# Transposed modulation parts, full-height score operands and head pairs in a two-layer hybrid backbone

## The chip, the cores and the metric

The kernel runs on one core of a Trainium2 chip. The metric is the device time of one execution in microseconds; the median of three runs of the kernel before is 2051.74 us (2051.34 to 2056.99).

## The reference, cut to what matters

The model takes 512 latent tokens and 256 context tokens of width 1024 through two layers. Each layer multiplies and shifts its input by rows that come from a conditioning vector, mixes tokens, normalises, and sends each token to two of 32 experts. The even layer mixes with a bidirectional linear recurrence beside windowed attention (8 query heads of 64, 2 key and value heads, a sink); the odd layer with latent attention (8 heads of 96, 64 for values) beside a depthwise convolution.

```python
def _modulation(cond, w, b):
    m = (jax.nn.silu(cond) @ w + b)[..., None, :]
    return jnp.split(m, 6, axis=-1)

def _modulate(x, shift, scale):
    return x * (1.0 + scale) + shift

# even layer, latent tokens: window of 128 each way, all context keys, one sink
p = jax.nn.softmax(jnp.concatenate([s_win, s_ctx, s_sink], axis=-1), axis=-1)
out = jnp.einsum('bnkgqm,bnmkd->bnqkgd', p_win, vb) + jnp.einsum('bnkgqc,bckd->bnqkgd', p_ctx, v_ctx)
# even layer, context tokens: all context keys and the sink
# odd layer: keys of context and latent tokens, every head of its own
p = jax.nn.softmax(s, axis=-1).astype(v.dtype)
return jnp.einsum('bhqk,bkhd->bqhd', p, v)
```

## The kernel before, in words

**Order.** `forward` (line 1659) runs the even mixer, its output projection and routing, the experts of layer 0, the odd mixer, and the same again. Instructions are written in program order; a planner, which simulates the engines with its own costs, lays out each engine's queue at compile time: it takes ready instructions by priority, the order of writing. On the chip every engine then works through its queue in order. Weights come in pieces of 2 MB through one queue (SP) into a ring of slots (`Stream`); a slot's next transfer starts when the work on it has ended (`done`).

**Modulation.** A section (one of six rows of 1024 per layer and per stream) is computed in two halves. `modulation_rows` (line 213) multiplies the two conditioning columns, padded to 32, with the weights. The contraction over 1024 is cut into four parts, each on its own 32 output partitions, so partition 32c holds part c for the latent stream and 32c+1 for the context. ScalarE copies that bank to SBUF (line 222). `modulation` (line 226) does both halves and gives back `finish`, which is called later: 16 matmuls (line 239) take 64 strided columns of the copy as the weights and `pick`, a 128x2 selector, as the moving operand, so that each adds the four parts and turns 64 features onto partitions. VectorE adds the bias (line 240). Ten sections go this way, six in the even mixer (`fill`, line 495) and four in the odd one (line 1983); the first two sections of layer 0 go through lines 361 to 368 with the same `modulation_rows`. Every f32 matmul in the program is two instructions in the trace, each with its own weight load.

**Heads of the even layer.** `maxima` (line 552) finds each query's row maximum and turns its negative, split into a bf16 pair, onto four partitions, `mT` (line 586). `scores` (line 614) makes one block of scores, keys on partitions: two f32r matmuls with the split queries and keys, one bf16 matmul that adds the maxima (`sel`, four rows, against `mT`, line 637; line 627 for the context's queries), and masks; ScalarE takes exp into a tile `P` (line 643; nine such tiles). `heads` (line 646) takes a pair of heads, t, which share the output banks `ol` and `oc`, head i on partitions 64i to 64i+63. It runs head 0's seven units and then head 1's. `use` multiplies P with the values (line 669, line 661 for the context's queries) two units after the scores, and GpSimd adds P into the head's first P tile (lines 674, 662). `normalise` (line 685) sums over keys with a matmul of ones (line 692), both heads side by side in one bank, adds the sink (line 693), and scales. The loop at line 705 calls it for the pair before, at the eighth step of the next pair.

**Heads of the odd layer.** `operands` (line 1901) makes each head's split queries `qh`, `ql` and keys `kh`, `kl`: 96 rows, and in `qh` and `kh` two more that carry the maxima and ones. The tiles alternate between two pools. `scores` (line 1996) uses 96, 96 and 98 rows (lines 1999 to 2001); lines 1935 and 1940 make the scores for the maxima with 96 rows.

Of the kernel before, what the change touches and what calls it, by code (L numbers as in the profile page):

```python
# [11 lines left out]
F = mybir.dt.float32  # L12
FR = mybir.dt.float32r
# [21 lines left out]
def host_arrays(inp):  # L35
# [6 lines left out]
    a["xT"] = x.reshape(NT, 8, 128).transpose(2, 1, 0)  # L42
    a["wmod"] = i["w_mod"].reshape(2, 128, 8, 12, 512).transpose(0, 3, 1, 2, 4).reshape(2, 12, 128, 4096)
    a["lng"], a["lnb"] = i["ln_g"], i["ln_b"]
# [71 lines left out]
    cf["pick"][0::32, 0] = cf["pick"][1::32, 1] = 1  # L116
    cf["eps"] = np.full((128, 1), EPS)
    F_off, o = {}, 0
    for k, v in cf.items():
# [92 lines left out]

def modulation_rows(K, s):

    nc = K.nc
    q = K.ps.tile([128, 512], F, tag="b", name="qmod")
    for k in range(2):
        for c in range(4):
            nc.tensor.matmul(q[32 * c:32 * c + 32], K.cond[:, 2 * c + k, :],  # L219
                             s[0][:, 1024 * c + 512 * k:1024 * c + 512 * k + 512], start=(k == 0), stop=(k == 1))  # L220
    m = K.mp.tile([128, 512], F, tag="msb", name="msb", bufs=2)
    nc.scalar.activation(m, q, AF.Copy)
    return m


def modulation(K, l, sec):

    nc = K.nc
    ms = []
    for b in range(2):  # L230
        s = K.stream.get(("mod", l, sec, b))
        ms.append(modulation_rows(K, s))
        K.stream.done(s)

    def finish():
        t = K.ps.tile([128, 512], F, tag="b", name="fmp")
        for b in range(2):
            for j in range(8):
                nc.tensor.matmul(t[64 * b:64 * b + 64, 2 * j:2 * j + 2], ms[b][:, j::8], K.cst["pick"], start=True, stop=True)
        nc.vector.tensor_tensor(K.fm[:, l, :, sec], t[:, 0:16].rearrange("p (j i) -> p i j", j=8),  # L240
                                K.fmb[:, l, None, sec].to_broadcast([128, 2, 8]), op=ALU.add)

    return finish
# [47 lines left out]
def mixer_even(K):  # L291
# [260 lines left out]
    def maxima(t):  # L552
# [31 lines left out]
        for b in range(6):  # L584
            PE.transpose(q[0:4, 128 * b:128 * b + 128], nb[:, b, :], c["identb"])
        mT = up.tile([4, 768], BF, tag="mT", name="mT", bufs=2)
        V.tensor_copy(mT, q[0:4, 0:768])
        early.append((qs, mT))
# [25 lines left out]
    def scores(h, qs, mT, unit_):  # L614
# [4 lines left out]
        p = ap.tile([128, 512], F, tag="P", name="P", bufs=9)  # L619
        sel = c["sel"][0:4, 128 * par:128 * par + 128]  # L620
        if kind == "x":
# [24 lines left out]
    def heads(t, qs, mT):  # L646
        kv = t // 2
        ol, oc = ps("ol"), ps("oc")
        sums = []
        for i in range(2):  # L650
            h = 2 * t + i
            r = slice(64 * i, 64 * i + 64)
            vs = lambda n: v[:, n, 64 * kv:64 * kv + 64]
            units = [("c", 0), ("w", 0), ("w", 1), ("w", 2), ("w", 3), ("c", 1), ("x", 0)]
            pend, first = [], []

            def use(u, p):
                kind, j = u
                if kind == "x":
                    for jj in range(2):  # L660
                        PE.matmul(oc[r, 0:256], vs(4 + jj), p[:, 256 * jj:256 * jj + 256], start=(jj == 0), stop=(jj == 1))
                    G.tensor_add(p[:, 0:256], p[:, 0:256], p[:, 256:512])
                    sums.append((first[0], p))
                    return
                if kind == "c":
                    vt, r0, r1 = 4 + j, 0, NL
                else:
                    vt, r0, r1 = j, max(0, 128 * j - 128), min(NL, 128 * j + 256)
                PE.matmul(ol[r, r0:r1], vs(vt), p[:, 0:r1 - r0], start=(u == ("c", 0)), stop=(u == ("c", 1)),
                          skip_group_check=True)  # L670
                if u == ("c", 0):
                    first.append(p)
                else:
                    G.tensor_add(first[0][:, r0:r1], first[0][:, r0:r1], p[:, 0:r1 - r0])

            for u in units:
                pend.append((u, scores(h, qs[i], mT, u)))
                if len(pend) > 2:
                    use(*pend.pop(0))
                yield  # L680
            for e in pend:
                use(*e)
        yield (ol, oc, sums)

    def normalise(t, mT, ol, oc, sums):
# [3 lines left out]
        for o, s, n, r0, m0 in ((ol, 0, 512, 0, 0), (oc, 1, 256, C0, 512)):  # L689
            dn, es = ps("dn"), ps("es")  # L690
            for i in range(2):
                PE.matmul(dn[64 * i:64 * i + 64, 0:n], c["onesf"][:, 0:64], sums[i][s][:, 0:n], start=True, stop=True)
            PE.matmul(es[:, 0:n], c["sel"][0:4, 256:384], mT[:, m0:m0 + n], start=True, stop=True)
            e = ap.tile([128, 512], F, tag="es", name="es", bufs=2)
# [10 lines left out]
    for t in range(4):  # L705
# [4 lines left out]
        for n, r in enumerate(heads(t, qs, mT)):  # L710
            if n % 2:
                next(mx, None)
            if n == 7 and last:
                normalise(*last)
            if n == 10 and t:
                for m in mix[2 * t - 2:2 * t]:
                    mixp.insert(len(mixp) - t, parts(m, 0, [slice(0, W)]))
# [950 lines left out]
def mixer_odd(K, uh, hh, hl):  # L1668
# [232 lines left out]
    def operands(h, w):  # L1901
# [11 lines left out]
        V.tensor_add(f[64:96], f[64:96], r[64:96])  # L1913
        pool = ap if h % 2 else op
        qh = pool.tile([98, NL], FR, tag="qh", name="qh")
        ql = pool.tile([96, NL], FR, tag="ql", name="ql")
        S.activation(qh[0:96], f, AF.Copy)
        V.tensor_sub(ql, f, qh[0:96].bitcast(F))
        if h < 2:
            khs[h] = pool.tile([98, W], FR, name="kh%d" % h)  # L1920
        kh = khs[h % 2]
        kl = pool.tile([96, W], FR, tag="kl", name="kl")
        for q, (s0, s1) in zip(kq, both):
# [9 lines left out]
        for b in range(4):  # L1933
            q = ps("mx")
            PE.matmul(q, qh[0:96, 128 * b:128 * b + 128], kh[0:96, 0:NL], start=True, stop=True)
            V.tensor_reduce(mx[:, b, 0:1], q, axis=AX.X, op=ALU.max)
        for b in range(0, 4, 2):
            q = ps("mx")
            for i in range(2):
                PE.matmul(q[:, 256 * i:256 * i + 256], qh[0:96, 128 * (b + i):128 * (b + i) + 128], kh[0:96, C0:W],  # L1940
                          start=True, stop=True)
# [54 lines left out]
    def scores(kh, kl, qh, ql):  # L1996
        for n, tk in enumerate(toks):
            q = ps("s")
            PE.matmul(q, kh[0:96, tk:tk + 128], ql, start=True, stop=False)
            PE.matmul(q, kl[:, tk:tk + 128], qh[0:96], start=False, stop=False)  # L2000
            PE.matmul(q, kh[:, tk:tk + 128], qh, start=False, stop=True)
# [204 lines left out]
def setup(ctx, tc, a, pvo, cfo, cbo):  # L2206
# [20 lines left out]
    def prologue(K):  # L2227
# [8 lines left out]
        K.cst = dict(ident=f("ident"), onesf=f("ones"), iota=f("iota"), iota2=f("iota2"), down=f("down"), tokc=f("tokc"),  # L2236
                     zero=f("zero"), pick=f("pick"), eps=f("eps"), tri=g("tri"), ones=g("ones"), identb=g("ident"), mge=g("mge"),
                     mle=g("mle"), sel=g("sel"))
# [40 lines left out]
```

## Time and profile before

| | us |
|---|---|
| median of three runs | 2051.74 |
| profiled execution, its own time | 2062.3 |
| its span, first to last instruction | 2060.5 |
| TensorE busy (88% of the span) | 1810.0 |
| VectorE busy | 911.9 |
| GpSimd busy | 481.9 |
| ScalarE busy | 471.7 |
| mean granted TensorE clock | 0.92 |

PE is TensorE's matmuls, PEld its weight loads, DVE VectorE, ACT ScalarE, POOL GpSimd. Busy times are of the one profiled execution. [...] The durations of matmuls overlap, so starts tell more than lengths. In the layout of the time, the even mixer takes the first 374 us, its projection and routing run to about 500, layer 0's experts to about 1040, the odd mixer to about 1420, and layer 1's experts to the end.

### The profile page before, as it was taken

The page shows a single profiled execution, that of the slowest core. Times are in us where ns is not written, and L with a number is a line of the kernel's source. Part 1 is how long each engine was busy: PE and PEld are TensorE (multiplying, and loading weights), DVE is VectorE, ACT ScalarE, POOL GpSimd, SP SyncE. Part 2 cuts the span into 40 slices and gives each one's busy share as a digit, 9 for nine tenths or more (in the row PEclk, how much of TensorE's full clock was granted, in tenths as well). Part 3 has the DMA queues.
Part 4 walks back from the last instruction along what each step waited for, and adds up shares of the span by engine and source line. Part 5 has one row for each costly group of instructions (what it writes and reads, how often), then busy time and mean ns, then how long its engine had stood idle before and what let it go on. Part 6 is the DMA issues. An engine that isn't in the chain of part 4 may idle for free. (4 is left out here: it accounts for less than half of the span.)

```text
span 2060.5 us, 23254 instructions
## 1 busy us (share of the span) xinstructions
PE 1810.0 (88%) x8514; PEld 950.9 (46%) x8515; DVE 911.9 (44%) x1631; ACT 471.7 (23%) x794; POOL 481.9 (23%) x415
## 2 busy tenths in 40 slices
PE   5999999995998989999967787999769999998785
PEld 3668644684333333333335663556633333333232
DVE  3676531577221221222167888465833233322127
ACT  3472322322010110101035453334310000000001
POOL 2142335333000000100033656334100010000103
PEclk9989898996999999999988797889879999999997
DMA  8741320426698999998982112424559999999973
GB/s 350 274 156 42 123 85 1 164 102 256 264 426 371 411 425 424 408 395 349 373 334 92 41 42 110 175 83 187 225 214 423 427 404 400 424 424 425 424 311 150
DMA packets 59023, 551.87 MB, mean 268 GB/s; under 512 B 13295, under 2 KB 13807, under 8 KB 28018
## 3 DMA queue, kind: packets, MB, share of 16 engines
q1 hardware_dynamic: 43490, 514.47, 61.1%
q0 software_dynamic: 11056, 21.00, 2.7%
q10 hardware_dynamic: 4320, 14.31, 1.8%
q8 instruction: 98, 1.61, 0.3%
q14 instruction: 59, 0.48, 0.1%
HBM read 535.00 MB, written 33.61 MB: 276 GB/s over the span
## 5 line engine op out<-in xcount | busy, mean ns | idle before, releaser
L916 PE MATMUL q<-ring,xT 128*64 128x512 f32 x1024 | 475.6, 608 | 43.5 <-PEq L1148 27.9
L917 PE MATMUL q<-ring,xT 128*64 128x512 f32 x1024 | 476.6, 609 | 5.6 <-DMA ring<-in_w_dram 5.6
L945 PE MATMUL q<-ring,hT 128*64 128x512 f32 x1152 | 297.6, 605 | 24.8 <-DMA ring<-in_w_dram 10.9
L916 PEld LDWEIGHTS q<-ring,xT 128*64 128x64 f32 x1024 | 132.3, 139 | 296.4 <-issue 264.6
L925 ACT ACTIVATE sl<-q 64x512 f32<-64x512 f32 x72 | 42.6, 592 | 752.1 <-PE q L917 742.4
L878 POOL DMA_INDIRECT xg<-f,tok x38 | 39.1, 1029 | 591.3 <-DVE tok L873 402.9
L945 PEld LDWEIGHTS q<-ring,hT 128*64 128x64 f32 x1152 | 88.7, 138 | 180.5 <-issue 167.4
L917 PEld LDWEIGHTS q<-ring,xT 128*64 128x64 f32 x1024 | 132.9, 139 | 28.5 <-issue 18.7
L935 DVE COPY hT<-q 128x256 f32<-128x256 f32 x72 | 30.6, 425 | 232.2 <-PE q L933 231.8
L263 PE MATMUL pj<-hh,wlo 128*128 128x512 f32 (+2 forms) x336 | 107.3, 371 | 12.9 <-DVE wlo L252 12.9
L263 PE MATMUL pj<-hl,whi 128*128 128x512 f32 (+2 forms) x336 | 105.0, 364 | 0.0
L263 PE MATMUL pj<-hh,whi 128*128 128x512 f32 (+2 forms) x336 | 104.6, 365 | 0.0
L1815 POOL TENSOR_TENSOR acc<-acc,prod 128x512 f32<-128x512 f32 x56 | 86.5, 1545 | 54.9 <-ACT prod L1814 52.0
L851 DVE TENSOR_TENSOR oh<-cf,pos 128x512 fp32r<-128x512 f32 (+1 forms) x65 | 53.3, 823 | 98.8 <-PE qi L865 97.8
L953 DVE TENSOR_TENSOR y<-q,m 64x512 f32<-64x512 f32 x70 | 48.2, 689 | 83.3 <-PE q L945 75.1
L891 DVE COPY xT<-qx 128x512 f32<-128x512 f32 x32 | 22.1, 692 | 123.2 <-PE qx L887 123.2
L956 DVE COPY y<-q 64x512 f32<-64x512 f32 x37 | 25.7, 693 | 113.9 <-ACT y L955 75.8
L926 DVE SCALAR_TENSOR_TENSOR h<-q,gate,sl 64x512 f32<-64x512 f32 x68 | 51.0, 749 | 56.4 <-ACT sl L925 35.4
L263 PEld LDWEIGHTS pj<-hh,wlo 128*128 128x128 f32 (+1 forms) x336 | 58.4, 195 | 28.9 <-DVE wlo L252 15.1
L1810 DVE SCALAR_TENSOR_TENSOR acc<-glu,pv,acc 128x512 f32<-128x512 f32 x60 | 70.9, 1187 | 0.9
L219 PE MATMUL qmod<-ring,cond 128*32 128x512 f32 x384 | 61.9, 786 | 10.6 <-ACT cond L2241 10.6
L916 PE MATMUL q<-ring,xTo 128*64 128x512 f32 x128 | 61.7, 639 | 8.0 <-DVE xTo L900 8.0
(523 smaller groups left out, 3144.1 us busy)
## 6 DMA issues: line engine op xcount, KB each, us to landing
ring<-in_w_dram SPq DMA_DIRECT2D x192, 2048.0 KB, 18.7
ring<-in_wmod_dram SPq DMA_DIRECT2D x24, 2048.0 KB, 8.7
ring<-Y SPq DMA_DIRECT2D x8, 1024.0 KB, 9.3
ring<-in_ew_dram SPq DMA_DIRECT2D x3, 2048.0 KB, 14.9
f<-t ACTq DMA_DIRECT2D x10, 512.0 KB, 3.3
xhat<-xh ACTq DMA_DIRECT2D x9, 512.0 KB, 3.7
ring<-in_ewo_dram SPq DMA_DIRECT2D x2, 2048.0 KB, 10.1
ring<-in_ow_dram SPq DMA_DIRECT2D x2, 2048.0 KB, 10.2
```

Of the source, the lines that this page charges most:

```text
L219: nc.tensor.matmul(q[32 * c:32 * c + 32], K.cond[:, 2 * c + k, :], s[0][:, 1024 * c + 512 * k:1024 * c + 512 * k + 512], start=(k == 0), s ...
L263: nc.tensor.matmul(q[0:m, 0:s1 - s0], a[:, k, 0:m], b[k][:, s0:s1], start=(k == i == 0), stop=(k == 7 and i == 2))
L851: V.tensor_tensor(oh.rearrange("p t (n s) -> p t n s", n=n), iota[:, None, None, :].to_broadcast([128, T, n, 64]), pos[:, :, e:e + n, None ...
L878: return G.indirect_dma_start(out=x[0:m], out_offset=None, in_=K.f, in_offset=bass.IndirectOffsetOnAxis(ap=tok[0:m], axis=0), bounds_check ...
L916: PE.matmul(q[a:a + 64], xT[:, k, :], w1[:, 512 * k:512 * k + 512], start=(k == 0), stop=(k == 7))
L917: last = PE.matmul(q[b:b + 64], xT[:, k, :], w3[:, 512 * k:512 * k + 512], start=(k == 0), stop=(k == 7)).ins
L925: S.activation(sl[a:a + 64], q[a:a + 64], AF.Silu)
L926: V.scalar_tensor_tensor(h[a:a + 64], q[b:b + 64], gate[a:a + 64], sl[a:a + 64], op0=ALU.mult, op1=ALU.mult)
L945: K.last_mm = PE.matmul(q[64 * o:64 * o + 64], hT[:, k, :], w2[:, 1024 * k + 512 * o:1024 * k + 512 * o + 512], start=(k == 0), stop=(k == ...
L953: V.tensor_mul(y[:, b], q[a], K.m5[a, b])
L1810: V.scalar_tensor_tensor(y, g[:, k:k + NL], w(k), y, op0=ALU.mult, op1=ALU.add)
L1815: G.tensor_add(z, z, p)
```

## The change

**Modulation.** For the ten sections, the halves' bank is no longer copied by ScalarE: VectorE transposes it in blocks of 32x32, so that 32 features of a block stand on partitions, once per part. `finish` multiplies with `stack`, four identities of 32 on top of each other, as the weights: 8 matmuls with 8 moving columns, on four groups of 32 output partitions. The host orders the columns of the weights for this; the first two sections of layer 0 keep the old way.

**Even heads.** `mT` has 128 rows, zeroed by GpSimd before VectorE writes four of them, and `sel` is read with all its 128 rows (zero beyond four). A unit is now computed for both heads before the next; the products of a unit follow the scores of the next unit, head 0's beside head 1's. `normalise` of the pair before is called at the fourth step.

**Odd heads.** All four operands have 128 rows, in tiles made for the first two heads and used again in turn; GpSimd zeroes rows 96 to 127 once, and rows 96 and 97 of `qh` for each later head. All matmuls on them read 128 rows.

```diff
-    a["wmod"] = i["w_mod"].reshape(2, 128, 8, 12, 512).transpose(0, 3, 1, 2, 4).reshape(2, 12, 128, 4096)
+    wm = i["w_mod"].reshape(2, 128, 8, 12, 512).transpose(0, 3, 1, 2, 4)
+    wp = i["w_mod"].reshape(2, 128, 8, 6, 4, 32, 2, 4).transpose(0, 3, 6, 1, 2, 4, 7, 5).reshape(2, 12, 128, 8, 512)
+    first = (np.arange(24).reshape(2, 12) < 4)[:, :, None, None, None]
+    a["wmod"] = np.where(first, wm, wp).reshape(2, 12, 128, 4096)
...
+    cf["stack"] = np.tile(np.eye(32), (4, 1))
...
-        ms.append(modulation_rows(K, s))
+        q = modulation_parts(K, s)
         K.stream.done(s)
+        m = K.mp.tile([128, 512], F, tag="msb", name="msb", bufs=2)
+        nc.vector.transpose(m, q)
+        ms.append(m.rearrange("p (n y) -> p n y", y=32))
...
-            for j in range(8):
-                nc.tensor.matmul(t[64 * b:64 * b + 64, 2 * j:2 * j + 2], ms[b][:, j::8], K.cst["pick"], start=True, stop=True)
+            for g in range(4):
+                nc.tensor.matmul(t[32 * g:32 * g + 32, 8 * b:8 * b + 8], K.cst["stack"], ms[b][:, 4 * g:4 * g + 4, 0:2],
+                                 start=True, stop=True)
...
-        mT = up.tile([4, 768], BF, tag="mT", name="mT", bufs=2)
-        V.tensor_copy(mT, q[0:4, 0:768])
+        mT = up.tile([128, 768], BF, tag="mT", name="mT", bufs=2)
+        G.memset(mT, 0.0)
+        V.tensor_copy(mT[0:4], q[0:4, 0:768])
...
-        sel = c["sel"][0:4, 128 * par:128 * par + 128]
+        sel = c["sel"][:, 128 * par:128 * par + 128]
...
+        both = [(i, slice(64 * i, 64 * i + 64)) for i in range(2)]
+        def use(u, pp):
...
+            for i, r in both:
+                PE.matmul(ol[r, r0:r1], vs(vt), pp[i][:, 0:r1 - r0], start=(u == ("c", 0)), stop=(u == ("c", 1)),
                           skip_group_check=True)
+            for i, p in enumerate(pp):
                 if u == ("c", 0):
                     first.append(p)
                 else:
+                    G.tensor_add(first[i][:, r0:r1], first[i][:, r0:r1], p[:, 0:r1 - r0])
+        pend = None
+        for u in [("c", 0), ("w", 0), ("w", 1), ("w", 2), ("w", 3), ("c", 1), ("x", 0)]:
+            pp = []
+            for i in range(2):
+                pp.append(scores(2 * t + i, qs[i], mT, u))
+                if i == 0:
+                    yield
+            if pend:
+                use(*pend)
+            pend = u, pp
+            yield
+        use(*pend)
...
-            if n == 7 and last:
+            if n == 3 and last:
                 normalise(*last)
...
+        if h < 2:
+            pool = ap if h else op
+            khs[h] = [pool.tile([128, n], FR, name="%s%d" % (nm, h)) for nm, n in (("kh", W), ("kl", W), ("qh", NL), ("ql", NL))]
+            for x in khs[h]:
+                G.memset(x[96:128].bitcast(F), 0.0)
+        kh, kl, qh, ql = khs[h % 2]
+        if h > 1:
+            G.memset(qh[96:98].bitcast(F), 0.0)
...
-            PE.matmul(q, qh[0:96, 128 * b:128 * b + 128], kh[0:96, 0:NL], start=True, stop=True)
+            PE.matmul(q, qh[:, 128 * b:128 * b + 128], kh[:, 0:NL], start=True, stop=True)
...
-            PE.matmul(q, kh[0:96, tk:tk + 128], ql, start=True, stop=False)
-            PE.matmul(q, kl[:, tk:tk + 128], qh[0:96], start=False, stop=False)
+            PE.matmul(q, kh[:, tk:tk + 128], ql, start=True, stop=False)
+            PE.matmul(q, kl[:, tk:tk + 128], qh, start=False, stop=False)
             PE.matmul(q, kh[:, tk:tk + 128], qh, start=False, stop=True)
```

## Rows read from the trace of the kernel before

**Rows 1.** Windows by stage; columns: window, length, busy per engine, clock, DMA share, GB/s.
```profile
60.00:160.00 100.00, 98.15 (x572) 70.14 (x561) 73.29 (x72) 66.53 (x94) 31.09 (x33) 0.93 0.51 201
226.00:374.00 148.00, 146.20 (x622) 67.15 (x620) 44.63 (x63) 48.29 (x89) 66.03 (x70) 0.86 0.15 59
346.00:374.00 28.00, 28.00 (x116) 11.70 (x115) 6.76 (x6) 12.02 (x24) 17.87 (x18) 1.00 0.02 3
500.00:1040.00 540.00, 495.93 (x2286) 197.70 (x2286) 128.06 (x279) 54.72 (x93) 46.72 (x47) 0.97 0.93 383
1276.00:1420.00 144.00, 137.29 (x688) 81.56 (x688) 79.09 (x130) 52.18 (x99) 51.27 (x43) 0.86 0.28 106
```

**Rows 2.** Windows around the stretches with a low clock, columns as in the first group.
```profile
120.00:153.00 33.00, 31.15 (x168) 21.75 (x168) 22.01 (x20) 23.70 (x32) 17.30 (x18) 0.79 0.44 161
233.00:276.00 43.00, 42.26 (x180) 20.49 (x184) 11.33 (x22) 12.03 (x22) 17.25 (x16) 0.76 0.18 75
312.00:334.00 22.00, 22.00 (x53) 8.84 (x52) 0.18 (x1) 3.54 (x7) 9.11 (x16) 0.53 0.00 1
1278.00:1314.00 36.00, 35.54 (x199) 18.56 (x198) 12.74 (x29) 9.43 (x19) 10.15 (x9) 0.76 0.35 132
1329.00:1367.00 38.00, 35.22 (x173) 20.60 (x174) 18.55 (x33) 11.08 (x23) 11.93 (x14) 0.78 0.29 112
```

**Rows 3.** Weight loads of the tiles `qmod` and `fmp`; durations minimum/median/maximum in ns.
```profile
L219 PEld LDWEIGHTS qmod<-ring,cond x384: 106/111/178, 10.6 to 1333.6; 128*32 128x32 f32 x192
...
L239 PEld LDWEIGHTS fmp<-cf,msb x320: 194/217/218, 71.5 to 1360.5; 128*64 128x64 f32 x160
```

**Rows 4.** Timeline of TensorE, runs of line 239; columns: start, length in us, instruction.
```profile
118.45 3.55 PE L239 MATMUL fmp<-cf,msb 128*64 128x2 f32 x32
...
308.81 3.55 PE L239 MATMUL fmp<-cf,msb 128*64 128x2 f32 x32
...
1325.79 3.55 PE L239 MATMUL fmp<-cf,msb 128*64 128x2 f32 x32
```

**Rows 5.** Timeline at 227 us, weight loads of a modulation.
```profile
227.33 0.19 PEld L219 LDWEIGHTS qmod<-ring,cond 128*32 128x32 f32 x4 [0.24 <-issue]
```

**Rows 6.** Groups of VectorE in 60 to 400 us.
```profile
L488 DVE STREAM_SHUFFLE sh<-qf 128x512 f32<-128x512 f32 x4 | 3.0, 745 | 0.0
```

**Rows 7.** Groups of TensorE in 226 to 374 us; busy us, mean ns.
```profile
L669 PE MATMUL ol<-P,v 128*64 128x512 f32 (+2 forms) x96 | 45.8, 581 | 0.0
...
L661 PE MATMUL oc<-P,v 128*64 128x256 f32 x32 | 8.9, 404 | 0.0
```

**Rows 8.** Timeline of TensorE from 308 us, two heads and one head.
```profile
334.10 1.08 PE L692 MATMUL dn<-P,cf 128*64 128x512 f32 x4
...
346.46 1.07 PE L669 MATMUL ol<-P,v 128*64 128x512 f32 x2
```

**Rows 9.** Groups of GpSimd in 226 to 374 us.
```profile
L674 POOL TENSOR_TENSOR P<-P 128x256 f32<-128x256 f32 (+2 forms) x40 | 37.8, 945 | 49.2 <-ACT P L643 32.8 <-PE ol L669 15.3
```

**Rows 10.** Timeline at 242 and 255 us, matmuls and weight loads together.
```profile
242.42 0.15 PEld L572 LDWEIGHTS <-cb 128*128 128x128 bf16 x1 [0.20 <-issue]
...
242.55 0.31 PE L574 MATMUL mw<-cb 128*128 128x128 bf16 x1
242.55 0.34 PEld L635 LDWEIGHTS st<-qs,k 128*128 128x128 f32 x1
...
255.03 0.38 PE L637 MATMUL st<-mT,cb 4*128 4x512 bf16 x1
255.34 0.30 PEld L561 LDWEIGHTS mc<-k,qs 128*128 128x128 f32 x2 [0.23 <-issue]
```

**Rows 11.** Timeline at 1409 us, matmuls and weight loads of the second layer's scores.
```profile
1409.84 0.40 PE L2000 MATMUL s<-qh,kl 96*128 96x512 f32 x1
1409.84 0.19 PEld L2001 LDWEIGHTS s<-qh,kh 98*128 98x128 f32 x1
```

**Rows 12.** Groups of GpSimd in 1190 to 1420 us.
```profile
L1928 POOL MEMSET kh<- 2x772 f32 x2 | 1.7, 858 | 0.1
```

More of the change, by code (lines that the diff above doesn't have):

```diff
@@ L210, in cols, with modulation_parts @@
     return K.pv[:, o:o + w]
-def modulation_rows(K, s):
+def modulation_parts(K, s):
     nc = K.nc
@@ L220, in modulation_rows @@
                              s[0][:, 1024 * c + 512 * k:1024 * c + 512 * k + 512], start=(k == 0), stop=(k == 1))
+    return q
+def modulation_rows(K, s):
+    q = modulation_parts(K, s)
     m = K.mp.tile([128, 512], F, tag="msb", name="msb", bufs=2)
-    nc.scalar.activation(m, q, AF.Copy)
+    K.nc.scalar.activation(m, q, AF.Copy)
     return m
@@ L231, in modulation @@
         s = K.stream.get(("mod", l, sec, b))
-        ms.append(modulation_rows(K, s))
+        q = modulation_parts(K, s)
         K.stream.done(s)
+        m = K.mp.tile([128, 512], F, tag="msb", name="msb", bufs=2)
+        nc.vector.transpose(m, q)
+        ms.append(m.rearrange("p (n y) -> p n y", y=32))
     def finish():
@@ L649, in heads @@
         sums = []
[L650 to L661, printed above, removed]
-                    G.tensor_add(p[:, 0:256], p[:, 0:256], p[:, 256:512])
[L663 to L669, printed above, removed]
+        vs = lambda n: v[:, n, 64 * kv:64 * kv + 64]
+        both = [(i, slice(64 * i, 64 * i + 64)) for i in range(2)]
+        first = []
+        def use(u, pp):
+            kind, j = u
+            if kind == "x":
+                for jj in range(2):
+                    for i, r in both:
+                        PE.matmul(oc[r, 0:256], vs(4 + jj), pp[i][:, 256 * jj:256 * jj + 256], start=(jj == 0), stop=(jj == 1),
+                                  skip_group_check=True)
+                for i, p in enumerate(pp):
+                    G.tensor_add(p[:, 0:256], p[:, 0:256], p[:, 256:512])
+                    sums.append((first[i], p))
+                return
+            if kind == "c":
+                vt, r0, r1 = 4 + j, 0, NL
+            else:
+                vt, r0, r1 = j, max(0, 128 * j - 128), min(NL, 128 * j + 256)
+            for i, r in both:
+                PE.matmul(ol[r, r0:r1], vs(vt), pp[i][:, 0:r1 - r0], start=(u == ("c", 0)), stop=(u == ("c", 1)),
                           skip_group_check=True)
+            for i, p in enumerate(pp):
                 if u == ("c", 0):
@@ L673, in use @@
                 else:
[L674 to L682, printed above, removed]
+                    G.tensor_add(first[i][:, r0:r1], first[i][:, r0:r1], p[:, 0:r1 - r0])
[11 more added lines that the diff above has]
+        use(*pend)
         yield (ol, oc, sums)
@@ L692, in normalise @@
                 PE.matmul(dn[64 * i:64 * i + 64, 0:n], c["onesf"][:, 0:64], sums[i][s][:, 0:n], start=True, stop=True)
-            PE.matmul(es[:, 0:n], c["sel"][0:4, 256:384], mT[:, m0:m0 + n], start=True, stop=True)
+            PE.matmul(es[:, 0:n], c["sel"][:, 256:384], mT[:, m0:m0 + n], start=True, stop=True)
             e = ap.tile([128, 512], F, tag="es", name="es", bufs=2)
@@ L1913, in operands @@
         V.tensor_add(f[64:96], f[64:96], r[64:96])
-        pool = ap if h % 2 else op
-        qh = pool.tile([98, NL], FR, tag="qh", name="qh")
-        ql = pool.tile([96, NL], FR, tag="ql", name="ql")
-        S.activation(qh[0:96], f, AF.Copy)
[L1918 to L1922, printed above, removed]
+        if h < 2:
[6 more added lines that the diff above has]
+            G.memset(qh[96:98].bitcast(F), 0.0)
+        S.activation(qh[0:96], f, AF.Copy)
+        V.tensor_sub(ql[0:96], f, qh[0:96].bitcast(F))
         for q, (s0, s1) in zip(kq, both):
@@ L1939, in operands @@
             for i in range(2):
-                PE.matmul(q[:, 256 * i:256 * i + 256], qh[0:96, 128 * (b + i):128 * (b + i) + 128], kh[0:96, C0:W],
+                PE.matmul(q[:, 256 * i:256 * i + 256], qh[:, 128 * (b + i):128 * (b + i) + 128], kh[:, C0:W],
                           start=True, stop=True)
@@ L2236, in prologue @@
         K.cst = dict(ident=f("ident"), onesf=f("ones"), iota=f("iota"), iota2=f("iota2"), down=f("down"), tokc=f("tokc"),
-                     zero=f("zero"), pick=f("pick"), eps=f("eps"), tri=g("tri"), ones=g("ones"), identb=g("ident"), mge=g("mge"),
+                     zero=f("zero"), pick=f("pick"), eps=f("eps"), stack=f("stack"), tri=g("tri"), ones=g("ones"), identb=g("ident"), mge=g("mge"),
                      mle=g("mle"), sel=g("sel"))
```

## The prediction

> **What bounds the kernel now.** I read the windows by stage first, then the groups of TensorE by line, then the timeline of TensorE with its weight loads. The reader is to see three things.
>
> First, the expert stages are bound by transfers and the mixers are not: in 500 to 1040 us the DMA engines are 93% busy at 383 GB/s [rows 1]. In the first mixer, 60 to 160 and 226 to 374 us, the DMA share is 0.51 and 0.15 while TensorE is busy for 98.15 of 100 and 146.20 of 148 us; in the second layer's heads it is busy for 137.29 of 144 us [rows 1]. The streams wait there for ring slots that the work frees, so what a mixer gains should move everything behind it forward by as much.
>
> Second, a busy TensorE is not a fast one: the granted clock is 0.86 in both head stages [rows 1]. Five stretches hold nearly all of the loss that matters here [rows 2]. [...]
>
> Third, six falls of the clock come within four microseconds of the start of a run of line 239, 32 matmuls of two columns, each behind a weight load of 0.217 us [rows 3]: the first run of the six at 118.45, the last at 1325.79, each 3.55 us long [rows 4]. There are ten such runs; behind two the clock holds, and before two it has fallen already. The run at 308.81 is the dearest: 22 us at 0.53 follow [rows 2, 4].
>
> **The change part by part.** Durations are from the profiled execution: span 2060.5 us, its own time 2062.3. The median of the three runs shown is 2051.74, 10.6 us less; I take the gain off the median.
>
> *Modulation.* Ten of the twelve sections go through `modulation`. Each run of 32 instructions on 64 columns with a strided weight read becomes 16 on a 32-column operand (two per f32 product, as before). The nearest row for such a load is line 219: 0.111 us alone [rows 3], and four of them, for four column groups, in 0.19 us [rows 5]. So 16 cost between 0.8 and 1.8 us, plus about 0.2 to drain; I take 1.5, nearer the upper end because the four groups here share one weight tile but alternate their moving data. Saved: 3.55 - 1.5 = 2.05, times ten = 20.5 us, bounds 15 and 26. All lie in stretches where TensorE is full. In exchange, 20 ScalarE copies become 20 VectorE transposes out of PSUM. The trace has no transpose there; the nearest is a shuffle of the same shape, 3.0 us for four [rows 6], though between SBUF tiles, so 0.75 each (bounds: half and double of it), 15 us in all. VectorE is 73% and ScalarE 67% busy in 60 to 160 [rows 1], so I count only two sections as landing on a full VectorE: -3 us (bounds 0 and -15).
>
> *Heads in pairs.* The products with the values (lines 669 and 661) use half of the output columns each and are busy for 45.8 + 8.9 = 54.7 us [rows 7]. What two halves do when they stand side by side is shown by line 692: four instructions of 512 columns, one head on each half, take 1.08 us, as long as two instructions of one head on line 669, 1.07 us [rows 8]. So a pair costs what one costs: at most 27 us off. Some of the 54.7 is at half clock (also in the clock term), and some products already overlap others, so I take 22. The lower bound is 0, if pairs don't end up adjacent. Exp of the second head must be ready before its product; two score groups of the next unit lie between, so it should be. GpSimd's additions don't change in number: 40 at 0.945 us plus eight smaller ones [rows 9]. In the last 28 us of the stage GpSimd is busy for 17.87 [rows 1], and TensorE will need some 8 us less there, so the two come close: -3 us for waits.
>
> *128-row operands, first layer.* Columns don't change, so the matmuls don't. Their weight loads do: behind the 4-row matmul at 255.03 the next load starts at 255.34, after the matmul's stream, whereas behind the 128-row bf16 matmul at 242.55 the next load starts with it, at 242.55 [rows 10]. A bf16 load behind an f32 matmul waits in either form (242.42, idle 0.20) [rows 10], so only the load after is freed: some 0.1 us (a bf16 or 64-column load) to 0.19 (a full f32 one), for 64 score operands and 8 of the normalisation: I take 7 us, bounds 0 and 13.7. [...]
>
> *128-row operands, second layer.* Here the load for the 98-row matmul already starts together with the 96-row matmul before it, at 1409.84 [rows 11]; nothing to free, 0 us on TensorE. GpSimd gets the memsets: 2 x 772 elements took 0.858 us [rows 12], so by length about 2 x (2 x 0.86 + 2 x 0.57) + 6 x 0.57 = 9 us in the odd layer and 4 x 0.86 at most in the even one. The odd ones of head 1 fall where GpSimd holds the convolution's sums; the maxima wait for them. That cover is mostly there, because VectorE is behind anyway: -1 us (bounds 0 and -3).
>
> *The clock.* Shorter column-poor runs, full-width product pairs and wider operands all put more of the array to work. [...]
>
> Sum: 20.5 - 3 + 22 - 3 + 7 - 1 + 15 = 57.5 us off, 2062.3 to 2004.8 in the profile, 2051.7 to 1994 in the median.
>
> **Rivals.**
> *The clock stays up.* Half-clock stretches behind line 239 nearly vanish: 30 us more, about 1964. For it: the six falls that follow such a run [rows 2, 4]. Against it: the run is followed by `qmod` matmuls or 128-column pieces that stay.
> *Pairs that aren't pairs.* The order on TensorE is laid out by a planner that puts whatever is ready between two products, or GpSimd and ScalarE set the pace of the stage. Then the 22 us and half of the clock's 15 go: 58 - 22 - 7 = 29 off, about 2023. For it: GpSimd at 17.87 of 28 [rows 1]. Against it: the second product's operand is two score groups old.
> *The ring of nine tiles.* Slower. Two heads at once want ten P tiles (four of the block before, two running sums, two waiting, two new) and there are nine until `normalise` lets go. If TensorE waits at each of five units in four blocks for two additions of 0.945 us, that is 20 x 1.9 = 38 us; with such gaps the stage would stay at half clock for perhaps 60 us more, another 30. Against gains of some 49 without the clock's this gives +19, about 2071. It decides from about 2.5 us of wait per unit. Against it: `normalise` moves up to the second unit of the next block, before the tenth tile is asked for.
>
> **How the numbers follow.** Forecast as summed, 1977 to 2011: 0.45. Clock stays up, 1945 to 1977: 0.20. Pairs lost or paced by others, 2011 to 2045: 0.20. Gains and waits cancel: 0.07. Ring of nine or another new wait, slower: 0.08. The likeliest time is 1994. The range 1952 to 2037 leaves out the slower cases and the ends of the rivals, about two in ten. A measurement here can tell 0.3%, 6 us, from no change: faster 0.86, same 0.06, slower 0.08 (cancelling is put mostly with no change).
>
> **What would show it.** The run at line 239's place takes 1.5 us, not 3.55. Products of two heads start within hundredths of a microsecond of each other, and the stage from 226 to 374 is some 40 us shorter with a clock above 0.86. The load after a `sel` matmul starts with it. The transposes take about 0.75 us each. The expert stages keep their lengths and only move. The forecast is wrong if TensorE shows idle gaps on GpSimd or ScalarE between unit pairs, if the expert stages start earlier but end where they did, or if the granted clock of the heads doesn't change and the sum still holds.

## The result, and the profile after

The changed kernel takes 1984.82 us (median of 4 runs, 1983.45 to 1988.28); the kernel before took 2054.36 us beside it (2051.34 to 2060.47). The ratio is 0.966, with a 95% interval of 0.9632 to 0.9689. Forecast were 1994 us, 1952 to 2037. The profiled spans are 2060.5 and 1982.3 us, 78.2 us apart.

Three stages of the kernel before hold nearly all of that. Their windows, cut at what is the same work in both kernels: from 60 us to the first score of the first layer's heads, from there to the first output projection, and the second layer's heads from the first score to the start of the last product. The first windows are rounded; the first scores stand at 230.5 and 217.2 us. Columns as in [rows 1].

```profile
60.00:230.00 170.00, 167.81 (x1008) 129.05 (x996) 118.41 (x138) 84.62 (x120) 50.97 (x43) 0.96 0.37 144
230.50:373.90 143.40, 141.60 (x580) 65.10 (x578) 42.09 (x62) 45.91 (x85) 64.08 (x69) 0.86 0.15 59
1227.40:1416.10 188.70, 166.68 (x788) 97.72 (x787) 125.32 (x186) 71.95 (x138) 84.29 (x66) 0.83 0.26 101
```

The same stretches of the kernel after, between the second and the last an expert stretch as in [rows 1], moved forward by 58 us:

```profile
60.00:217.00 157.00, 149.19 (x917) 114.59 (x914) 122.18 (x144) 76.88 (x107) 51.22 (x43) 0.98 0.39 155
217.20:317.10 99.90, 95.89 (x543) 48.66 (x547) 50.24 (x66) 42.85 (x81) 66.16 (x72) 1.00 0.21 84
442.00:982.00 540.00, 496.08 (x2269) 196.98 (x2268) 127.92 (x279) 54.64 (x92) 46.68 (x47) 0.96 0.93 381
1168.80:1338.20 169.40, 144.43 (x724) 80.78 (x723) 135.63 (x195) 67.57 (x131) 89.61 (x76) 0.89 0.29 112
```

The stages are 13.3, 43.5 and 19.3 us shorter, 76.1 of the 78.2. The expert stretch reads as before to a unit: 496 of 540 us of TensorE, 93% of the DMA engines. What the mixers gained went through to the end.

The clock column divides the gain. At any one moment the granted clock of both profiles reads 1.00 or 0.50, so of w us with a mean of c, 2w(1-c) are half-clock time. At 0.50 the 512-column matmuls of line 263 of the kernel before start 0.427 us apart and the 8-column ones of line 865 0.213, at 1.00 0.231 and 0.112 (medians): about half of the half-clock time is lost. Before: 170 x 0.04 x 2 = 13.6, 143.4 x 0.14 x 2 = 40.2, 188.7 x 0.17 x 2 = 64.2. After: 6.3, 0 and 37.3. So 3.7 + 20.1 + 13.4 = 37 us of the 76.1 are clock, and 39 us are fewer or better overlapped instructions. Leaving out the half-clock time in which TensorE was idle changes the 37 by less than 1 us. The same sum over the whole program, at mean clocks of 0.920 and 0.934, gives 34.

Now the pieces. The first group is the modulation's run and the transposes that feed it (durations minimum/median/maximum in ns); it answers to [rows 4] and [rows 6].

```profile
L253 PE MATMUL fmp<-msb,cf x160: 172/186/223, 69.9 to 1284.3; 128*32 128x8 f32 x160
...
L246 DVE STREAM_TRANSPOSE msb<-qmod x20: 668/705/717, 58.4 to 1263.2; 128x512 f32<-128x512 f32 x20
```

The timeline shows such a run whole: its 16 instructions begin at 273.45 and have ended by 273.82.

```profile
273.45 0.21 PE L253 MATMUL fmp<-msb,cf 128*32 128x8 f32 x3
273.50 0.32 PE L253 MATMUL fmp<-msb,cf 128*32 128x8 f32 x13
```

That is under 0.4 us in place of 3.55. The timeline of the scores, matmuls and weight loads together, answers to [rows 10]: line 653 is the mask operand, now of 128 rows, and the load behind it starts with it.

```profile
231.50 0.28 PE L653 MATMUL st<-mT,cb 128*128 128x256 bf16 x1
231.51 0.10 PEld L656 LDWEIGHTS <-cb 128*128 128x128 bf16 x1
```

This is no single case: behind 42 such matmuls of the first layer's heads the next load starts 0.011 us after the matmul in the median; behind 38 of the 4-row form in the kernel before, at full clock, it starts 0.260 us after.

The products with the values, as groups of 217 to 317 us (busy us, mean ns), against 45.8 and 8.9 us in [rows 7]:

```profile
L687 PE MATMUL ol<-P,v 128*64 128x512 f32 (+2 forms) x96 | 30.5, 509 | 0.4 <-issue 0.4
...
L676 PE MATMUL oc<-P,v 128*64 128x256 f32 x32 | 6.7, 392 | 0.0
```

And as a timeline: a pair that is adjacent (x4, 0.87 us for two heads), and, from 260.81, products that stand alone (x2, 0.86 us for one) with the maxima of another head (line 576) put between.

```profile
229.64 0.87 PE L687 MATMUL ol<-P,v 128*64 128x384 f32 x4
...
260.81 0.86 PE L687 MATMUL ol<-P,v 128*64 128x384 f32 x2
261.60 0.50 PE L576 MATMUL mc<-k,qs 128*128 128x256 f32 x2
262.03 0.86 PE L687 MATMUL ol<-P,v 128*64 128x384 f32 x2
```

Some 11 of the 24 pairs of line 687 are adjacent. The reader is to see that "their products are adjacent" holds in the program's text, and for half of them on the engine.

### The profile page after: what moved, and what is told of

Its sections match the earlier page's. It is cut to its first block, busy times and chain, and to the rows that moved or that the text cites. A ratio compares the mean times of both kernels' runs of the same rounds, so it can differ in the third digit from the quotient of the medians.

```text
span 1982.3 us, 22945 instructions
## 1 busy us (share of the span) xinstructions
PE 1723.8 (87%) x8347; PEld 901.1 (45%) x8355; DVE 934.8 (47%) x1651; ACT 459.0 (23%) x774; POOL 495.2 (25%) x433
## 5 line engine op out<-in xcount | busy, mean ns | idle before, releaser
L969 PE MATMUL q<-ring,hT 128*64 128x512 f32 x1152 | 300.2, 610 | 24.1 <-DMA ring<-in_w_dram 10.2
L984 POOL DMA_INDIRECT Y<-y,idx x33 | 32.8, 993 | 147.1 <-DVEq L1172 71.7
L957 PEld LDWEIGHTS q<-cf,h 64*128 64x128 f32 x288 | 39.8, 209 | 59.3 <-issue 55.8
## 6 DMA issues: line engine op xcount, KB each, us to landing
ring<-in_wmod_dram SPq DMA_DIRECT2D x24, 2048.0 KB, 10.6
```

The lines of the kernel that those rows point to most:

```text
L957: last = PE.transpose(q[:, 64 * j:64 * j + 64], h[a:a + 64, j:512:4], c["ident"][a:a + 64, a:a + 64]).ins
L969: K.last_mm = PE.matmul(q[64 * o:64 * o + 64], hT[:, k, :], w2[:, 1024 * k + 512 * o:1024 * k + 512 * o + 512], start=(k == 0), stop=(k == ...
```

## The experiments

Two theories at first. A: the ten column-poor runs of the modulation (matmuls with few moving columns) set the clock. B: what the heads' own matmuls fill sets it. An old run is the 32 instructions of two columns, a new run the 16 of eight. The parts of the change were built one by one, each from the kernel before. Gains in us are the ratio's share of the time of the kernel before beside each (2059.97 us for these four).

**The modulation alone.** Lines 224 to 255 with the host's reordering of `w_mod`; the rest as before.

```
...
-                nc.tensor.matmul(t[64 * b:64 * b + 64, 2 * j:2 * j + 2], ms[b][:, j::8], K.cst["pick"], ...)
+                nc.tensor.matmul(t[32 * g:32 * g + 32, 8 * b:8 * b + 8], K.cst["stack"], ms[b][:, 4 * g:4 * g + 4, 0:2], ...)
```

> The kernel before with the modulation part alone. Theory A (the runs of two-column matmuls set the clock): ten runs shrink from 3.55 to about 0.4 us of their own, 25 to 30 us off, and without the long runs the clock of 226 to 374 us rises from 0.86 to 0.95 or more: 40 to 55 us off in all, about 2000 to 2012. Theory B (what the heads' own matmuls fill of the array sets the clock): the runs' price alone, 20 to 30 us off, about 2025, and the clock falls to 0.50 in the heads again, for stretches as long as before.

Measured: 2005.96 us, ratio 0.9743 (0.967 to 0.9817), 53 us off, the time of theory A. The clock of the heads rose to 0.92, not to A's 0.95, and a fall of some 20 us stayed in them (the row is below).

**The pairs alone.**

```
-        for i in range(2):
-            h = 2 * t + i
...
+            for i, r in both:
+                PE.matmul(ol[r, r0:r1], vs(vt), pp[i][:, 0:r1 - r0], ...)
```

> The kernel before with the head pairs alone. Theory A: 15 to 20 us off (the products' price, busy 54.7 us to about 37), the clock of the head stage stays near 0.86 and the fall behind the run of line 239 at about 309 us stays: about 2033. Theory B: the clock comes back sooner behind each fall, because product pairs fill both halves; 30 to 40 us off, about 2016. If pairs brought a new wait (the ring of nine): slower than 2051.

Measured: 2045.46 us, ratio 0.9929 (0.9893 to 0.9964), 14.6 us off: hardly what A gave the products, half of what B forecast. But the clock of the heads rose to 0.94, which A did not have.

**The 128-row operands of the first layer alone.**

```
...
-        sel = c["sel"][0:4, 128 * par:128 * par + 128]
+        sel = c["sel"][:, 128 * par:128 * par + 128]
...
```

> The kernel before with the 128-row operands of the first layer alone. Theory A: the freed weight loads, 5 to 10 us off, about 2044. Theory B: a half-clock stretch in the heads lasts under 10 us instead of 17 and 20, 15 to 25 us off, about 2031. [...]

Measured: 2035.56 us, ratio 0.9898 (0.9851 to 0.9946), 21 us off, as B had it.

**The 128-row operands of the second layer alone.**

```
...
-            PE.matmul(q, qh[0:96, 128 * b:128 * b + 128], kh[0:96, 0:NL], start=True, stop=True)
+            PE.matmul(q, qh[:, 128 * b:128 * b + 128], kh[:, 0:NL], start=True, stop=True)
...
```

> The kernel before with the 128-row operands of the second layer alone. Theory A: no change within 3 us (2048 to 2055); no weight load is freed there. Theory B: the clock of 1276 to 1420 us rises from 0.86 to 0.92 or more, 8 to 15 us off, about 2040.

Measured: 2055.23 us, ratio 0.998 (0.9958 to 1.0002): not told from no change, as A had it.

The parts sum to some 93 us; together they gave 70. With the intervals of the four ratios that is 93, give or take some 19, so the times alone barely show that the parts share something. What they share is seen in the window of the first layer's heads, one row from each kernel in the order above:

```profile
220.80:349.40 128.60, 126.80 (x549) 55.83 (x546) 44.41 (x66) 44.14 (x82) 63.40 (x69) 0.92 0.16 66
```

```profile
235.10:358.10 123.00, 122.10 (x580) 57.47 (x579) 46.94 (x63) 45.22 (x84) 64.80 (x70) 0.94 0.18 72
```

```profile
232.50:352.70 120.20, 115.93 (x583) 59.81 (x579) 43.56 (x62) 45.13 (x85) 65.66 (x71) 0.96 0.18 70
```

```profile
230.20:367.50 137.30, 135.50 (x582) 62.63 (x579) 41.16 (x62) 45.80 (x85) 64.16 (x69) 0.90 0.16 62
```

Each of the first three raises the clock from 0.86 towards 1.00; after them all it can rise no further. Taken at full clock (length less half the half-clock time) the stage is 123.3 us before, 118.3 with the modulation, 115.6 with the pairs, 115.4 with the 128-row operands and 99.9 with all: the work adds up (5 + 7.7 + 7.9 = 20.6 against 23.4), the clock does not. The fourth row is a caution: its first-layer heads are those of the kernel before, line for line, with TensorE's instructions in the same order, and read 0.90, so 0.04 of clock is what one execution differs from another. At full clock it takes 123.6 us, as the kernel before does within 0.3.

That gave theory C, one pot of clock, and D, each part its own. The test was to take one part out of the kernel after.

**All but the 128-row operands of the first layer** (the edit above, reversed).

> Everything of the change but the 128-row score operands of the first layer. Theory C (one pot: the parts work on the same half-clock time of the heads, about 40 us at half clock, which is all gone in the kernel after; a part that is taken out costs its own work at full clock, here 8.5 us): about 1993 us, granted clock of the heads near 1.00. Theory D (each part brings its own clock, as when it stood alone, 21 us): about 2006, heads at 0.96 or lower again.

Measured: 1993.1 us, ratio 0.9687 (0.9647 to 0.9726).

**All but the pairs.**

> Everything of the change but the pairs. Theory C: it costs the pairs' own work, about 8 us: 1993, heads near clock 1.00. Theory D: 14.6 us as alone: 1999, with half-clock stretches back in the heads.

Measured: 1994.98 us, ratio 0.9688 (0.9648 to 0.9727).

**All but the modulation.**

> Everything of the change but the modulation: the runs of 32 two-column instructions are back. Theory C: the heads' own matmuls are now full enough to get the clock back within some ten us behind a run, so it costs the runs' own work (10 x 3.2 us less what is hidden) and little of the clock in the heads: 2010 to 2020. Theory D: 53 us as alone: about 2038, with twenty-microsecond falls behind the runs.

Measured: 2025.55 us, ratio 0.9838 (0.9789 to 0.9886).

The first two come within 2 us of C: against the kernel after, 8 and 10 us by the medians, where they had brought 21 and 14.6 alone. By the ratios it is 6 each, and the intervals overlap that of the kernel after, so for the pairs the times do not settle C against D. The clock of the heads speaks for C: 0.97 and 1.00 without the one and without the other, where D had 0.96 or lower and new half-clock stretches. The heads' windows of the three kernels, and of the last one the stretches around a run and the second layer's heads:

```profile
221.30:335.90 114.60, 113.73 (x550) 50.43 (x546) 49.46 (x67) 43.71 (x81) 64.75 (x70) 0.97 0.19 77
```

```profile
218.60:329.10 110.50, 105.74 (x540) 51.88 (x546) 46.15 (x66) 43.39 (x82) 65.54 (x71) 1.00 0.19 76
```

```profile
232.70:343.00 110.30, 105.58 (x573) 56.43 (x579) 49.21 (x62) 44.48 (x84) 66.18 (x72) 0.94 0.20 79
...
253.30:257.30 4.00, 3.08 (x21) 1.51 (x19) 3.47 (x4) 1.80 (x3) 3.84 (x3) 1.00 0.00 0
259.30:264.30 5.00, 5.00 (x38) 2.74 (x39) 0.17 (x1) 0.00 (x0) 0.48 (x1) 0.52 0.01 3
...
1191.00:1377.80 186.80, 164.46 (x787) 96.73 (x787) 129.41 (x187) 72.25 (x139) 88.94 (x76) 0.84 0.26 102
```

Without the modulation it came out between C and D: 41 us worse than the kernel after. By stages (first head score, heads, second layer) it is 15.5 + 10.4 + 17.4 = 43.3 us longer in the profile, of which 3.7 come back between the heads and the second layer, where nothing differs. So most of it lies outside the heads, where neither pairs nor 128-row operands of the first layer can give the clock back. The second layer's heads take 186.8 us, nearly the 188.7 of before: what they gained is the modulation's. The fourth and fifth rows are the four us ahead of one old run, at full clock, and five us from 2 us behind its start: 0.52.

I read all runs in this way, in all kernels but the last one below: of 36 old runs that began with the four us ahead at 1.00, 34 were followed by a clock of 0.76 or less; of 55 new ones, one. The fourth run of each kernel is a bad witness: the clock falls there in the new kernels too, ahead of the run, in a stretch where TensorE waits (in the kernel after it is idle for the four us from 130). Without it the old runs are 29 of 31, and the new ones remain 1 of 55. That is theory A, as far as the start of a fall goes.

How long a fall lasts is less clear. Behind the 34 old runs 32 falls last 3.4 or 6.8 us, one 10.2 and one 20.4. The heads have four long falls, of 17 to 20 us:

```profile
233.70:250.80 17.10, 17.06 (x45) 7.60 (x46) 4.08 (x7) 3.65 (x7) 6.51 (x6) 0.50 0.40 170
312.30:332.70 20.40, 20.40 (x46) 8.17 (x46) 0.18 (x1) 3.54 (x7) 8.08 (x15) 0.50 0.00 1
```

```profile
224.60:245.10 20.50, 20.50 (x52) 8.61 (x51) 5.16 (x9) 5.21 (x10) 8.34 (x7) 0.50 0.30 129
...
224.04 0.39 PE L576 MATMUL mc<-k,qs 128*128 128x256 f32 x1 [1.02 <-POOL qs L564]
```

```profile
291.10:308.20 17.10, 17.10 (x41) 6.75 (x41) 6.92 (x10) 4.95 (x10) 5.47 (x7) 0.50 0.00 0
311.60:318.40 6.80, 6.80 (x20) 2.67 (x19) 0.17 (x1) 1.47 (x3) 3.40 (x10) 0.50 0.00 0
```

Two are in the kernel before, one with the modulation alone, one with the second layer's operands alone: all in kernels with neither the pairs nor the 128-row operands of the first layer. In kernels with either the longest fall in the heads is 10.2 us (with the pairs alone, 302.9 to 313.1). That fits B. Only the one from 312.3 stands behind a run, so a fall needs none: the one from 224.6 began behind a wait of 1.02 us for GpSimd. But each is one execution, and the length of a single fall says little: behind the run at some 309 us, with TensorE's instructions in the same order, the clock was at half for 20.4 us in the kernel before and for 6.8 in that with the second layer's operands (last row).

**The pairs tied together.** Why are half of the pairs apart? Theory P: the planner puts other work between. Rival Q: the second operand is late. The kernel after; head 1's product first, head 0's tied behind it on TensorE, so that nothing can come between.

```
-            for i, r in both:
-                PE.matmul(ol[r, r0:r1], vs(vt), pp[i][:, 0:r1 - r0], start=(u == ("c", 0)), stop=(u == ("c", 1)),
-                          skip_group_check=True)
+            last = None
+            for i, r in both[::-1]:
+                with K.tc.issue_after(last) if last else nullcontext():
+                    last = PE.matmul(ol[r, r0:r1], vs(vt), pp[i][:, 0:r1 - r0], start=(u == ("c", 0)), stop=(u == ("c", 1)),
+                                     skip_group_check=True).ins
```

(and so for the products of line 676).

> The kernel after, with each pair's second product tied directly behind its first in the order on TensorE (head 1 first, then head 0). Theory P (about half of the 24 window pairs are apart only because the planner puts a score group or the maxima between them): all pairs overlap, products 37 -> some 28 us busy, 8 to 10 us off: about 1976. Rival Q (they are apart because the second operand is late): TensorE waits for Exp before a pair instead, and the time stays at 1985 or goes to 1995.

Measured: 1968.69 us, ratio 0.9564 (0.9525 to 0.9602). The same kernel once more, beside the next two:

> The kernel with the tied pairs again, as the companion of the next two: 1969 us, heads at clock 1.00.

Measured: 1961.25 us, ratio 0.9537 (0.9506 to 0.9569). It beats both kernels: 16 to 24 us under the one after by the medians, and its intervals end below the other's 0.9632. The second run's heads, groups and window:

```profile
L691 PE MATMUL ol<-P,v 128*64 128x512 f32 (+2 forms) x96 | 20.5, 509 | 0.3 <-issue 0.3
...
L678 PE MATMUL oc<-P,v 128*64 128x256 f32 x32 | 4.2, 385 | 0.2 <-ACT P L659 0.2
```

```profile
218.90:304.10 85.20, 82.31 (x542) 44.95 (x549) 48.65 (x67) 42.62 (x81) 65.71 (x72) 1.00 0.26 104
```

Products 24.7 us in place of 37.2, idle ahead of them half a us in all, and the stage 14.7 us shorter than in the kernel after. In the timeline all 24 pairs are adjacent. Theory P it is: the second operand had not been late. The gain is about double the 8 to 10 us forecast. Compared with the kernel without pairs (products 38.8 + 8.4 = 47.2 us, stage 110.5), pairs done fully are worth 25 us of stage; as the change has them, 10.6.

**Ten P tiles.** From the kernel with tied pairs, as are the next two.

```
-        p = ap.tile([128, 512], F, tag="P", name="P", bufs=9)
+        p = ap.tile([128, 512], F, tag="P", name="P", bufs=10)
```

> The kernel with tied pairs, and ten P tiles instead of nine. If the ring of nine never makes TensorE wait: 1969, within 3 us. If it does, as the rival with the ring had it: shorter by the waits, over 5 us.

Measured: 1966.47 us, ratio 0.9569 (0.9532 to 0.9607): no gain. The heads take 85.10 us, against 85.20; in this kernel the ring does not make TensorE wait.

**Denominators as products, second layer.** The column-poor run that is left.

```
-                    PE.matmul(dn[:, 4 * i + b:4 * i + b + 1], x[:, 128 * b:128 * b + 128], c["onesf"][:, 0:1], ...)
...
+                PE.matmul(dn[64 * i:64 * i + 64], c["onesf"][:, 0:64], x, ...)
...
+        V.reciprocal(r, dn)
+        yield
+        V.tensor_mul(r, r, o)
```

> The kernel with tied pairs, and in the second layer's attention the denominators worked out as in the first: per head pair, 16 one-column instructions, two transposes and 8 spreading instructions of 128 columns on TensorE become two products of 512 columns with a 64-column operand of ones, side by side, and the reciprocal of 8 columns becomes one of 512 on VectorE. If the column-poor run is what starts the half-clock stretch after it: the run's some 3.5 us per pair and up to 10 us of half clock go, VectorE has 2 to 3 us more per pair: about 1958. If the clock there falls because VectorE and GpSimd leave TensorE waiting: no clock back, VectorE 10 us longer where it sets the pace, 1968 to 1975.

Measured: 1978.53 us, ratio 0.9605 (0.9576 to 0.9634), 17 us slower than its companion. The second layer's heads of the companion, then of this kernel, and this kernel's timeline and VectorE group:

```profile
1151.20:1320.40 169.20, 144.15 (x724) 81.59 (x723) 136.23 (x195) 67.97 (x131) 88.96 (x76) 0.89 0.29 112
```

```profile
1162.30:1341.50 179.20, 144.97 (x651) 75.66 (x650) 139.76 (x192) 75.97 (x136) 89.84 (x76) 0.89 0.27 106
...
1271.71 1.08 PE L2041 MATMUL dn<-accp,cf 128*64 128x512 f32 x4 [1.76 <-DVE mx L1966]
...
1274.57 3.34 DVE L2045 RECIPROCAL rd<-dn 128x512 f32<-128x512 f32 x1
```

The time is above both forecasts. The clock is 0.89 in both kernels, so taking that run out gave none back, and the reciprocal takes 3.34 us of an engine that is already busy for 136 of 169. The stage is 10.0 us longer. Another 11 us lie ahead of it (it starts at 1162.3, not 1151.2), 9.5 of them between the heads and here, where nothing was edited and where the profiles of all kernels differ by as much (844 to 857 us). The profiled execution is the slowest of its four, so these 11 are no effect of the edit that could be shown. Profiles of one program differ by several us as well: the second layer's heads of the tied pairs, 169.2 us at 0.89 above, had been

```profile
1149.40:1325.50 176.10, 150.89 (x724) 85.58 (x723) 135.33 (x195) 67.99 (x131) 89.75 (x76) 0.85 0.28 108
```

when they were first measured.

**The new run ten times over.** Is it the length of the run, or its shape?

```
-            for g in range(4):
+            for g in list(range(4)) * 10:
```

> The kernel with tied pairs, and each of the modulation's ten runs written ten times over: 160 instructions of the new shape in place of 16, some 3 us long as the old run was, with the same result. If it is the length of the column-poor stretch that lets the clock fall: behind most of the runs that start at full clock the granted clock falls (in 34 of 36 old runs it did, in 1 of 55 new ones), the time rises by the ten runs (some 28 us) and the falls behind them, to 2000 or more. If it is the shape of the old run (two columns behind a full weight load): the clock stays, and the time rises by the runs alone, to about 1990.

Measured: 1990.36 us, ratio 0.9666 (0.9637 to 0.9696). The 160 instructions took 1.52 us, not 3 (70.88 below), so the test is half of what was meant.

```profile
70.88 1.52 PE L253 MATMUL fmp<-msb,cf 128*32 128x8 f32 x160
...
221.90:318.90 97.00, 90.04 (x836) 48.59 (x836) 50.12 (x67) 42.82 (x81) 65.66 (x72) 0.95 0.23 90
239.10:243.10 4.00, 4.00 (x31) 2.03 (x31) 3.65 (x5) 2.34 (x4) 3.92 (x4) 1.00 0.00 0
245.10:250.10 5.00, 3.19 (x16) 0.92 (x19) 0.00 (x0) 0.00 (x0) 0.90 (x2) 0.59 0.01 3
...
246.91 6.10 PE L224 MATMUL qmod<-ring,cond 128*32 128x512 f32 x25 [2.21 <-issue]
...
278.24 0.44 PE L600 MATMUL mT<-cb,nb 128*4 128x128 bf16 x5 [2.07 <-DVE nb L596]
```

Of eight runs that began at full clock two were followed by a fall, both in the first layer's heads; there were none behind the short runs of the kernel with tied pairs in its heads. That may be the length. But at both TensorE also stood idle as it did not with the short runs: for 2.21 us behind the run at 243.1, for 2.07 us ahead of the run at 278.5 (last two rows). The time is what the other theory, the shape, had forecast, for runs twice as long. The ten runs themselves cost some 12 us, but the kernel 22 to 29 more than the two measurements with tied pairs; falls and waits around the runs are left for the rest, not divided. Whether length or shape starts the falls behind the old runs stays open.

## Why the prediction was right

The sum was 57.5 us, against 69.5 between the medians. The mechanisms held but for the pairs, of which only half came about; three sizes were off, and the two largest errors, the clock and the pairs, pull against each other. That the sum came within 12 us is in part luck.

*Modulation, 20.5 us and -3 for the transposes.* Right in kind. I priced 16 instructions at 1.5 us; they take under 0.4, so a run saves 3.2 instead of 2.05. My nearest row, four loads in 0.19 us [rows 5], was right, and adding a drain and an upper bound to it was not. A transpose takes 0.705 us, predicted 0.75. So ten runs save 32 us, but the work shows as 9.6 us ahead of the heads (13.3 less 3.7 of clock), some 5 in them and 5.9 in the second layer (19.3 less 13.4), about 20. The 20.5 came out by two errors: that all ten lie where TensorE is full was wrong too. TensorE's idle time rose from 2.2 to 7.8 us ahead of the heads, from 1.8 to 4.0 in them and from 22 to 25 in the second layer. The largest piece is ahead of the fourth run, which waits for ScalarE (kernel after, then before):

```profile
134.02 0.40 PE L253 MATMUL fmp<-msb,cf 128*32 128x8 f32 x16 [6.06 <-ACT g L453]
...
144.15 3.55 PE L239 MATMUL fmp<-cf,msb 128*64 128x2 f32 x32 [1.85 <-ACT g L438]
```

*Pairs, 22 us and -3 for waits.* The step that failed: the change does make a pair cost what one costs, 0.87 us, but half of the pairs are not adjacent. The products fell from 54.7 to 37.2 us busy, part of that by the clock; taken alone or taken out, the pairs are worth 7.7 to 10.6 us of the stage. I had named the mechanism as a rival ("a planner that puts whatever is ready between two products") and had priced it as all or nothing. The tied version shows the 22 to be what full pairs give: 25. The -3 for waits was about right: TensorE's idle time in the heads went from 1.8 to 4.0 us.

*128-row operands, first layer, 7 us.* Right: 7.9 us of work alone, 6 to 8 us when taken out; the ratio of this edit alone is 0.9898. The matmuls take as long as before: with 512 columns at full clock 0.385 us with 4 rows (line 637 of the kernel before) and 0.392 with 128 (line 653). The load behind the mask operand starts with it, as read in [rows 10]: 0.01 us after it at 231.50.

*Second layer, 0 and -1.* Right within the measurement: 0.998 (0.9958 to 1.0002).

*The clock, 15 us.* Mis-sized: no run shows this term; in its place the runs showed 34 to 37. In the heads all of the half-clock time went, 40 us of it, and 27 us of the second layer's 64. The runs, shrunk to 0.4 us, almost never start a fall (1 of 55), while the old ones did 29 times in 31. The fall from 233, which has no run ahead of it, went as well: the kernel after has no fall in its heads. And the five stretches of [rows 2] were not all that could come back: by 2w(1-c) they hold 89 us at half clock, the three stages 118, of which half is 59 us and not 44.6; most of the difference lies between 1227 and 1278. The rival "the clock stays up" (1964 us, 0.20) described the heads rightly. It did not hold in the second layer, which stays at 0.89. There VectorE is busy for 135.63 of 169.40 us and TensorE is idle for 25; in the four us ahead of the six falls there TensorE was busy for 0.56 to 3.45 us. That its waits cause these falls was not tested.

So the clock gave some 20 us more than the sum said and the pairs some 12 less: 57.5 + 20 - 12 = 65.5, against 69.5 between the medians and 78.2 between the two profiled executions from which these sizes are read. What is left was not divided.

*The ring of nine* was wrong: the kernel after has no such wait in its heads, and with tied pairs a tenth tile changes nothing (heads of 85.10 us against 85.20). The 60 us at half clock behind such waits were an estimate of mine that no run shows.

## What to carry to other kernels

Judge a short column-poor run by the clock of the stretch behind it too: 3.55 us of such instructions brought falls of 3.4 or 6.8 us, rarely longer, and a run of 0.4 us nearly none. In one stage, gains that come through the clock are one pot, so that parts tried alone can promise more than they give together (here 93 us against 70); compare them at full clock. And where a pair must be adjacent on the engine, tie the two together and look at the timeline: program order gave half of the pairs, the tie gave the other half and 16 to 24 us. A single profile tells less than it seems to: one stage of one program took 169.2 and 176.1 us.

## What the runs showed of the hardware

- Sixteen f32 instructions of 8 columns in four column groups take 0.3 to 0.4 us in all, and 160 of them 1.52 us, under 10 ns each, though a load alone is 0.109 us (median of the 1600 loads in that kernel).
- A VectorE transpose of 32x32 blocks, 128x512 f32 out of PSUM, takes 0.705 us, about as long as a maximum over the same shape (0.677 us, second layer's heads).
- Behind a column-poor run of 3.55 us that began at full clock the granted clock fell to 0.50 in 29 of 31 cases (34 of 36 with a place where it falls in every kernel), for 3.4 or 6.8 us in all but two. Behind a run of 0.4 us it did in 1 of 55.
- The next weight load starts 0.011 us after a bf16 matmul with a 128-row operand, and 0.260 us after one with a 4-row operand (medians in the first layer's heads at full clock).
- The clock of the same instructions in the same order read 0.86 and 0.90 in the first layer's heads of two programs, 6 us of a 140 us stage, and 0.85 and 0.89 in the second layer's heads of one program, 7 us.
